# A two-layer hybrid encoder: another order of the mixer's steps, one load of x, TensorE in the order of the source

## The chip, the cores and the metric

The kernel runs on one core of a Trainium2 chip. The metric is the device time of one execution in microseconds. A core has five engines that run side by side and meet through semaphores: TensorE (PE, matrix products and transposes), VectorE (DVE), ScalarE (ACT), GpSimd (POOL) and SyncE (SP), which here only starts transfers. Products are accumulated in PSUM, in banks of 128 x 512 numbers.

## The reference

x is 256 positions of 1024 numbers. There are two layers, each of three stages, and all is float32:

```
x += 0.5 * SwiGLU(RMSNorm(x))             # FFN of width 2816
h  = RMSNorm(x); z = h @ W_in             # all projections of the mixer at once
y_att  = dilated window attention(zq, zk, zv)   # 8 heads of 64, q and k normed per head
y_pool = centred means of 2, 4, 8, 16 positions, less identity, a small map per group
y_rec  = recurrence in both directions (4 heads of 64), normed, times silu(hg)
x += concat(y_att, y_pool, y_rec) @ W_out
x += 0.5 * SwiGLU(RMSNorm(x))
```

The recurrence keeps a state S_t = diag(f_t) S_(t-1) + (1 - f_t) i_t^T with the output S_t^T q_t. Its gates f_t come from sigmoids of the projections, so the products of gates over a stretch of positions are needed.

## The kernel before

**Products.** Every product is made of three, since each number is split into a high and a low part that TensorE multiplies in full speed: high x high (L174), low x high or high x low (L175, L176). A product is 128 x 128 times 128 x 512. The weights come as halves of 512 KB in one long list, in the order of use. SP starts the transfer of a half into `stage`; ACT copies its high part `whi` (L149); DVE subtracts for the low part `wlo` (L151), or POOL does for the halves that POOL_HALVES lists. `ahead` splits a half four halves before its use, into a pool of five buffers, so that the copy of a half also waits until TensorE is done with the half five places before it.

**Stages.** An FFN goes over 11 blocks of 256 columns: `gate_up` makes gate and up for a block from four halves, `turn` transposes the product h (L352), `down` adds its part of the output. The last `down` of a stage works by quarters (dh, tt) of the residual, 128 x 512 each: six products, then DVE adds the quarter to x (`add`, L371), ACT sums its squares (L283), TensorE transposes it in four blocks (`turn`, L296, bank xps), and ACT and DVE split the transposes into `xh` (L274) and `xl` (L275) for the next stage. The turn of the last quarter is kept as `pending` and done after the first half of the next stage. The places where one stage ends and the next begins are called seams here; there are five.

**The mixer.** `mixer` runs through a string of steps, ORDER, one for each layer. c:n is chunk n of the input projection (c:2 to c:5 are q, c:6 to c:9 are k). mm:m are the products of level m of the recurrence (L541, bank lev): each level doubles the stretch over which positions meet, and up:m multiplies U and W by the gates' products in place on DVE (L520, L510), so mm of a level waits for up of the one before. put:m copies a level's result by a mask into A. ns:q scales q by its norm (DVE, L651, after the sums L644 and ACT's Ln and Exp, L645 and L646); nq:j and nk:j transpose q and k (L660, bank tp), sc and tr are the scores, pv the values' products, and o:name is a part of the output projection (L174 to L176, bank wo), the last of which goes by quarters and ends in a seam. rec and rnorm make the recurrence's output, and o:rec needs it.

**What sets the order.** SP takes its instructions in the order of the source (`manual_schedule`). For the other engines a planner orders them by its own estimate of when each will be ready, so a later-written product can stand ahead of an earlier-written transpose.

**Start.** x comes twice: as it is (for the residual) and transposed (`x_t`, four transfers of 256 KB into the space of `bias`), so that the first stage needs no transposes. In block 4 of the first FFN `setup` loads the tables of the masks and the attention bias and makes a product of them (L405, bank bps).

Of the kernel before, what the change touches and what calls it, by code (L numbers as in the profile page):

```python
# [16 lines left out]
P = 128  # L17
# [24 lines left out]
HALF = 1024  # L42
IN_NAMES = ("hq", "q", "k", "zh", "hg", "v")
OUT_NAMES = ("pool", "rec", "a0", "a1")
WIDE = ("q", "k", "zh", "v")
# [3 lines left out]
    (  # L49
# [4 lines left out]
    ),  # L54
    (
# [4 lines left out]
    ),  # L60
)
LOOK = 4
POOL_HALVES = ((3, 4, 5, 7, 8, 9, 12, 16, 20, 22, 24, 25, 27, 28, 29, 31), (2, 5, 6, 7, 8, 12, 16, 18, 19, 20, 21, 23, 24, 25, 26, 27, 28, 29, 31))
T2 = 10
FFN_HALVES = 6 * NB
# [5 lines left out]
class Trunk:  # L71
    def __init__(self, ctx, tc, x_in, xt_in, wall, prm_in, rel_in, cst_in, cst2_in, msk_in, band_in, y_out):
# [18 lines left out]
        self.pending = None  # L91
# [12 lines left out]
        self.xt0 = self.bias[:, 0]  # L104
        self.cp.tile([P, 16], F32, name="pad0")
        xr = xt_in.rearrange("p (k t) -> p k t", k=KC)
# [3 lines left out]
        for j in range(4):  # L110
            if j < 2:
                q = slice(j * HALF // 2, (j + 1) * HALF // 2)
                nc.sync.dma_start(w0[:, q], wall[0][:, q])
            nc.sync.dma_start(self.xt0[:, 2 * j:2 * j + 2, :], xr[:, 2 * j:2 * j + 2, :])
        self.feed_dma(2)
        self.prm_in, self.cst_in = prm_in, cst_in
        self.ident = self.cst[:, K_ID:K_ID + P]
        nc.scalar.dma_start(self.ident, cst_in[:, K_ID:K_ID + P])
        nc.scalar.dma_start(self.x, x_in.rearrange("p (t d) -> p t d", t=2))
# [38 lines left out]
    def ahead(self, i):  # L158

        self.feed_dma(i + LOOK + 4)  # L160
        self.feed_split(i + LOOK)

# [20 lines left out]
    def late_turn(self):  # L183

        if self.pending is not None:
            self.pending()
            self.pending = None

    def gate_up(self, i0, gu, mid=None):

        for q in range(4):
            if q == 1:
                self.late_turn()
            if q == 2 and mid is not None:
# [127 lines left out]
    def ffn(self, stage, post):  # L322
# [66 lines left out]

    def setup(self, after):  # L390
# [3 lines left out]
        mskf = self.mx.tile([P, 2 * len(LEVELS), 64], F32, tag="Kp", name="mskf", bufs=2)  # L394
        with self.tc.issue_after(after.ins):
# [53 lines left out]
    def mixer(self, l):  # L449
# [6 lines left out]
        def tl(tag, shape, dt=F32, **k):  # L456
            return mx.tile(shape, dt, tag=tag, name=tag, **k)
# [98 lines left out]
        def lev_put(m):  # L556
# [44 lines left out]
        def head_rs(sq, tag):  # L601

            ps = pg.tile([P, 512], F32, tag="g", name="hss")
            f = lambda t: t.rearrange("p a t -> p (a t)")
            hi, lo = self.split(sq)
            nc.tensor.matmul(ps, lhsT=self.bones, rhs=f(hi), start=True, stop=False)
# [5 lines left out]
            return rs  # L612

        def rec_norm():
            ops = V["ops"]
            sq = self.t2("sq")
            nc.scalar.activation(sq, ops, AF.Square)
            rs = head_rs(sq, "rrs")
            nc.vector.tensor_tensor(rs, rs, ops, op=ALU.mult)
# [162 lines left out]
        def out(nm):  # L782
# [21 lines left out]
    def body(self):  # L804
        nc = self.nc
        self.new_xt()
        for j in range(4):
            if j < 2:
                self.split_part(0, j * HALF // 2, (j + 1) * HALF // 2)
            for k in (2 * j, 2 * j + 1):  # L810
                self.parts(0, k, self.xt0[:, k, :])
# [54 lines left out]
def _pack(inp):  # L866
# [86 lines left out]
```

## Time and profile before

| | |
|---|---|
| median of three runs | 1042.7 us (1040.74 to 1046.78) |
| profiled execution | 1040.81 us, its span 1039.0 us |
| TensorE at work | 1004.4 us, 97% of the span |
| DVE, ACT, POOL | 585.0, 538.8 and 88.3 us |
| chain that ended last | TensorE 87%, DVE 6%, ACT 3%, issue 3%, DMA 1% |
| bytes moved | 182.20 MB, mean 175 GB/s |

TensorE is the engine to look at. A share of 97% includes stretches at the lower clock and a pipeline whose ends are modelled, so it is not TensorE at its peak. The waits tell where it stood, and the granted clock of a stretch tells where it was slow.

### The profile page before, as it was taken

What the parts mean: (1) busy time and instruction counts of PE and PEld (TensorE: products, weight loads), DVE (VectorE), ACT (ScalarE), POOL (GpSimd) and SP (SyncE); (2) the same over time, 40 slices, a digit from 0 to 9 for tenths busy, and PEclk for the clock granted to TensorE, in tenths of its full rate; (3) what the DMA queues carried; (4) which work ended last, traced back from release to release, by engine and by line L of the source; (5) the groups of instructions that cost most, each with busy time, mean ns of one, the idle gap of its engine ahead of it and who ended that gap; (6) DMA issues with size and microseconds to landing.
All of it is one profiled execution on the core that took longest, in us unless ns stands there. A gap on an engine that the chain in (4) does not pass through costs nothing.

```text
span 1039.0 us, 14421 instructions
## 1 busy us (share of the span) xinstructions
PE 1004.4 (97%) x5682; PEld 826.2 (80%) x5682; DVE 585.0 (56%) x776; ACT 538.8 (52%) x774; POOL 88.3 (8%) x43
## 2 busy tenths in 40 slices
PE   6999999998999999999999999999889999999998
PEld 4878888886867888888878888889768678888886
DVE  5655555669835555555565555554977155555553
ACT  7544444684865544444564444447648555444442
POOL 0000000140230000000000000004132400000000
PEclk9999999999999999999999999999989999999999
DMA  7769655553334555555555555554523346555551
GB/s 265 245 219 329 234 188 193 165 163 123 103 122 136 179 192 182 186 192 188 185 168 187 190 185 186 195 185 138 165 83 102 102 147 196 184 185 189 194 186 58
DMA packets 50420, 182.20 MB, mean 175 GB/s; under 512 B 5768, under 2 KB 6024, under 8 KB 49968
## 3 DMA queue, kind: packets, MB, share of 16 engines
q1 hardware_dynamic: 48528, 174.09, 51.6%
q0 software_dynamic: 720, 4.21, 1.1%
q10 hardware_dynamic: 1104, 2.99, 0.8%
q8 instruction: 44, 0.72, 0.3%
q14 instruction: 24, 0.20, 0.1%
HBM read 180.20 MB, written 3.16 MB: 176 GB/s over the span
## 4 chain that ended last, share of the span: by engine, by line
PE 87%; DVE 6%; ACT 3%; issue 3%; DMA 1%; POOL 0%; SPq 0%; ACTq 0%; DVEq 0%; POOLq 0%
PE gu L175 15%; PE gu L176 15%; PE gu L174 15%; PE ya L174 8%; PE ya L176 8%; PE ya L175 8%; PE hp L352 2%; PE wo L174 2%; PE wo L175 1%; PE wo L176 1%; ACT whi L149 1%; DVE wlo L151 1%; PE xps L296 1%; DMA bias<-x_t 1%; PE lev L541 1%
## 5 line engine op out<-in xcount | busy, mean ns | idle before, releaser
L149 ACT ACTIVATE whi<-stage 128x1024 fp32r<-128x1024 f32 (+1 forms) x329 | 347.1, 1056 | 395.3 <-PE gu L176 202.3
L151 DVE TENSOR_TENSOR wlo<-stage,whi 128x1024 fp32r<-128x1024 f32 (+1 forms) x294 | 360.7, 1229 | 337.5 <-ACT whi L149 337.4
L174 PE MATMUL gu<-whi,xh 128*128 128x512 f32 x704 | 275.7, 392 | 8.0 <-ACT xh L274 5.7
L175 PE MATMUL gu<-wlo,xh 128*128 128x512 f32 x704 | 274.9, 391 | 0.5 <-DVE wlo L151 0.5
L176 PE MATMUL gu<-whi,xl 128*128 128x512 f32 x704 | 274.7, 390 | 0.0
L174 PEld LDWEIGHTS gu<-whi,xh 128*128 128x128 f32 x704 | 132.5, 188 | 37.5 <-ACT xh L274 5.7
L175 PEld LDWEIGHTS gu<-wlo,xh 128*128 128x128 f32 x704 | 132.7, 189 | 28.7 <-DVE wlo L151 1.4
L176 PEld LDWEIGHTS gu<-whi,xl 128*128 128x128 f32 x704 | 132.6, 188 | 27.7
L174 PE MATMUL ya<-whi,hi 128*128 128x512 f32 x352 | 141.2, 401 | 0.0
L151 POOL TENSOR_TENSOR wlo<-stage,whi 128x1024 fp32r<-128x1024 f32 x35 | 85.0, 2437 | 654.5 <-ACT whi L149 639.2
L176 PE MATMUL ya<-whi,lo 128*128 128x512 f32 x352 | 137.8, 391 | 0.0
L175 PE MATMUL ya<-wlo,hi 128*128 128x512 f32 x352 | 137.4, 390 | 0.0
L176 PEld LDWEIGHTS ya<-whi,lo 128*128 128x128 f32 x352 | 66.1, 188 | 14.3
L175 PEld LDWEIGHTS ya<-wlo,hi 128*128 128x128 f32 x352 | 66.3, 188 | 12.4
L174 PEld LDWEIGHTS ya<-whi,hi 128*128 128x128 f32 x352 | 66.2, 188 | 12.3
L345 ACT ACTIVATE g<-gu,rc 128x256 f32<-128x256 f32 x88 | 41.5, 475 | 47.4 <-PE gu L176 47.4
L346 DVE SCALAR_TENSOR_TENSOR h<-gu,rc,g 128x256 f32<-128x256 f32 x88 | 42.0, 481 | 23.7 <-ACT g L345 23.7
L260 DVE TENSOR_TENSOR lo<-hp,hi 128x512 fp32r<-128x512 f32 x44 | 30.1, 684 | 2.8 <-ACT hi L259 2.8
L259 ACT ACTIVATE hi<-hp 128x512 fp32r<-128x512 f32 x44 | 25.6, 581 | 2.7 <-PE hp L352 2.7
L541 PE MATMUL lev<-U,W 64*64 64x64 f32 x384 | 15.6, 237 | 11.4 <-DVE W L520 11.4
L352 PEld LDWEIGHTS hp<-cst,h 128*128 128x128 f32 x176 | 21.8, 139 | 5.7
L352 PE MATMUL hp<-cst,h 128*128 128x128 f32 x176 | 26.3, 272 | 0.0
(224 smaller groups left out, 1035.8 us busy)
## 6 DMA issues: line engine op xcount, KB each, us to landing
stage<-w_all SPq DMA_DIRECT2D x327, 512.0 KB, 3.5
skew<-drow POOLq DMA_DIRECT2D x1, 2048.0 KB, 12.1
bias<-skew POOLq DMA_DIRECT2D x2, 1024.0 KB, 10.3
bias<-x_t SPq DMA_DIRECT2D x4, 256.0 KB, 7.9
x<-x ACTq DMA_DIRECT2D x1, 1024.0 KB, 8.4
band<-band ACTq DMA_DIRECT2D x1, 1024.0 KB, 8.0
y_t<-x SPq DMA_DIRECT2D x4, 256.0 KB, 2.2
stage<-w_all SPq DMA_DIRECT2D x2, 256.0 KB, 4.7
```

The source lines that it names most:

```text
L149: nc.scalar.activation(hi[:, s], st[:, s], AF.Copy)
L151: eng.tensor_tensor(lo[:, s], st[:, s], hi[:, s].bitcast(F32), op=ALU.subtract)
L174: nc.tensor.matmul(out, lhsT=ah, rhs=wh, start=start, stop=False, skip_group_check=True)
L175: nc.tensor.matmul(out, lhsT=ah, rhs=wl, start=False, stop=False, skip_group_check=True)
L176: nc.tensor.matmul(out, lhsT=al, rhs=wh, start=False, stop=stop, skip_group_check=True)
L259: self.nc.scalar.activation(hi, src, AF.Copy)
L260: self.nc.vector.tensor_tensor(lo, src, hi.bitcast(F32), op=ALU.subtract)
L296: nc.tensor.transpose(self.xps[k // 2][:, j % 2, tt * P:tt * P + P], self.x[:, tt, k * P:k * P + P], self.ident)
L345: silu = nc.scalar.activation(g2[:, tt, :], gu[tt][:, 0:256], AF.Silu, scale=r)
L346: nc.vector.scalar_tensor_tensor(h[:, tt, :], gu[tt][:, 256:512], r, g2[:, tt, :], op0=ALU.mult, op1=ALU.mult)
L352: nc.tensor.transpose(hp[:, f, tt * P:tt * P + P], h[:, tt, f * P:f * P + P], self.ident)
L541: nc.tensor.matmul(ps[d][e * 64:e * 64 + 64, hb * 64:hb * 64 + 64], lhsT=a, rhs=c, start=(hb == 0), stop=(hb == 7), skip_group_check=True)
```

## The change

1. In ORDER the steps of the mixer are placed anew: the levels are spread over more chunks, nq and nk come at other places, v's chunks come before hg's, o:rec comes last in place of o:a1, and rnorm is cut in two (rn1: squares and their split; rn2: the rest). T2, the number of buffers for small tiles, is 16.
2. x is loaded once, in quarters on SP's queue between the parts of the first half of the weights. The first stage is fed by transposes on TensorE. Twelve products of ones by ones (`idle`) stand ahead of them, the turn of the second part of x is `pending`, the squares are made later (`then`), and the halves are split no further ahead than `look`, which starts at 0.
3. TensorE is added to `manual_schedule`: its instructions keep the order of the source.
4. `setup` is cut into its loads (block 3) and its use (block 6); the tile Kp has one buffer.

```diff
-IN_NAMES = ("hq", "q", "k", "zh", "hg", "v")
-OUT_NAMES = ("pool", "rec", "a0", "a1")
+IN_NAMES = ("hq", "q", "k", "zh", "v", "hg")
+OUT_NAMES = ("pool", "a0", "a1", "rec")
...
-        "c:0 ga c:1 gb c:2 uv c:3 c:4 c:5 mm:0 ns:q put:0 mm:1 up:2 c:6 put:1 mm:2 up:4 c:7 put:2 nq:0 c:8 mm:4 up:8 nq:1 put:4 "
...
+        "c:0 ga c:1 gb c:2 uv c:3 c:4 c:5 mm:0 ns:q put:0 c:6 mm:1 up:2 put:1 nq:0 c:7 c:8 mm:2 up:4 nq:1 c:9 put:2 mm:4 up:8 ns:k "
...
-T2 = 10
+T2 = 16
...
+        for dh in range(2):
+            s = slice(dh * 512, dh * 512 + 512)
+            for tt in range(2):
+                nc.sync.dma_start(self.x[:, tt, s], xr[:, tt, s])
...
-        self.feed_split(i + LOOK)
+        self.feed_split(i + self.look)
...
+            if q == 3 and self.then is not None:
+                self.then()
+                self.then, self.look = None, LOOK
...
-            if b == min(4, NB - 1) and stage == 0:
-                self.setup(silu)
+            if b == 3 and stage == 0:
+                self.setup_loads(silu)
+            if b == 6 and stage == 0:
+                self.setup()
...
+        def rec_squares():
+            sq = self.t2("sq")
+            nc.scalar.activation(sq, V["ops"], AF.Square)
+            V["osq"] = self.split(sq)
...
+        idle = self.pg.tile([P, 512], F32, tag="g", name="idle")
+        for _ in range(12):
+            self.nc.tensor.matmul(idle[:, 0:P], lhsT=self.ones, rhs=self.ones, start=True, stop=True)
...
+        for tt in range(2):
+            self.turn(0, 0, tt)
+        self.feed_dma(5)
+
+        def second():
             for tt in range(2):
+                self.turn(0, 1, tt)
...
+        self.pending, self.then, self.look = second, sums, 0
...
-        ctx.enter_context(tc.manual_schedule(engines={mybir.EngineType.SP}))
+        ctx.enter_context(tc.manual_schedule(engines={mybir.EngineType.SP, mybir.EngineType.PE}))
```

TensorE at the seam behind layer 0's mixer, before (wo are the output projection's quarters, numbered in order; xps the banks of the transposes):

```order
L176 MATMUL wo_2839<-whi_2898,lo_2937 128x512
L174 MATMUL wo_2840<-whi_2916,hi_2936 128x512
L175 MATMUL wo_2840<-wlo_2917,hi_2936 128x512
L296 MATMUL xps_2994<-cst_85,x_83 128x128 x2
L296 MATMUL xps_2997<-cst_85,x_83 128x128 x2
L176 MATMUL wo_2840<-whi_2916,lo_2937 128x512
L296 MATMUL xps_2994<-cst_85,x_83 128x128 x2
L296 MATMUL xps_2997<-cst_85,x_83 128x128 x2
L174 MATMUL wo_2840<-whi_2916,hi_2936 128x512
L175 MATMUL wo_2840<-wlo_2917,hi_2936 128x512
L176 MATMUL wo_2840<-whi_2916,lo_2937 128x512
L174 MATMUL wo_2841<-whi_2916,hi_2936 128x512
```

and after:

```order
L175 MATMUL wo_2882<-wlo_2938,hi_2863 128x512
L176 MATMUL wo_2882<-whi_2937,lo_2864 128x512
L300 MATMUL xps_3025<-cst_85,x_83 128x128 x2
L300 MATMUL xps_3028<-cst_85,x_83 128x128 x2
L174 MATMUL wo_2883<-whi_2937,hi_2863 128x512
L175 MATMUL wo_2883<-wlo_2938,hi_2863 128x512
L176 MATMUL wo_2883<-whi_2937,lo_2864 128x512
L174 MATMUL wo_2883<-whi_2937,hi_2863 128x512
L175 MATMUL wo_2883<-wlo_2938,hi_2863 128x512
L176 MATMUL wo_2883<-whi_2937,lo_2864 128x512
L300 MATMUL xps_3025<-cst_85,x_83 128x128 x2
L300 MATMUL xps_3028<-cst_85,x_83 128x128 x2
```

Before, the transposes of the first two quarters came two products into the third quarter and one after the other; after, those of the first quarter stand behind its own sixth product (the first rows are its last), and six products later come those of the second.

TensorE in layer 1's mixer at the turn of q (tp from zq; k_ are chunks of k), before:

```order
L174 MATMUL k_6307<-whi_6183,xh_5845 128x512
L175 MATMUL k_6307<-wlo_6184,xh_5845 128x512
L176 MATMUL k_6307<-whi_6183,xl_5846 128x512
L660 MATMUL tp_6387<-cst_85,zq_6236 128x128
L660 MATMUL tp_6387<-cst_85,zq_6241 128x128
L660 MATMUL tp_6387<-cst_85,zq_6236 128x128
L660 MATMUL tp_6387<-cst_85,zq_6241 128x128
L174 MATMUL k_6306<-whi_6201,xh_5845 128x512
L175 MATMUL k_6306<-wlo_6202,xh_5845 128x512
```

and after (lev are the products of level 1):

```order
L552 MATMUL lev_6320<-U_6205,W_6206 64x64 x2
L552 MATMUL lev_6321<-W_6206,U_6205 64x64 x2
L674 MATMUL tp_6361<-cst_85,zq_6267 128x128
L674 MATMUL tp_6361<-cst_85,zq_6272 128x128
L674 MATMUL tp_6361<-cst_85,zq_6267 128x128
L674 MATMUL tp_6361<-cst_85,zq_6272 128x128
L174 MATMUL k_6300<-whi_6214,xh_5876 128x512
L175 MATMUL k_6300<-wlo_6215,xh_5876 128x512
L176 MATMUL k_6300<-whi_6214,xl_5877 128x512
```

Before, the turn followed chunk 7; now it comes between the products of level 1 and chunk 7.

ACT at that place (hs are the sums of the squares of q; L659 is Ln and L660 is Exp, L645 and L646 before), before:

```order
L149 ACTIVATE whi_6310<-stage_6156 128x1024
L643 ACTIVATE sq_6243<-zq_6241 128x512
L562 ACTIVATE A_6267<-lev_6248 128x512
L645 ACTIVATE hs_6235<-hs_6235,cols_108 128x16
L646 ACTIVATE hs_6235<-hs_6235 128x16
L149 ACTIVATE whi_6367<-stage_6181 128x1024
```

and after:

```order
L149 ACTIVATE whi_6304<-stage_6187 128x1024
L657 ACTIVATE sq_6274<-zq_6272 128x512
L573 ACTIVATE A_6298<-lev_6279 128x512
L659 ACTIVATE hs_6266<-hs_6266,cols_106 128x16
L149 ACTIVATE whi_6372<-stage_6212 128x1024
L660 ACTIVATE hs_6266<-hs_6266 128x16
```

A copy of a half, whi_6372, has come between Ln and Exp.

DVE there, before:

```order
L151 TENSOR_TENSOR wlo_6311<-stage_6156,whi_6310 128x1024
L644 TENSOR_REDUCE hs_6235<-sq_6243 128x8
L520 TENSOR_TENSOR U_6174<-U_6174,dw_6144 128x512
L520 TENSOR_TENSOR W_6175<-W_6175,dw_6144 128x512
L651 TENSOR_TENSOR zq_6236<-zq_6236,hs_6235 128x512
L651 TENSOR_TENSOR zq_6241<-zq_6241,hs_6235 128x512
```

and after:

```order
L151 TENSOR_TENSOR wlo_6305<-stage_6187,whi_6304 128x1024
L658 TENSOR_REDUCE hs_6266<-sq_6274 128x8
L151 TENSOR_TENSOR wlo_6373<-stage_6212,whi_6372 128x1024
L665 TENSOR_TENSOR zq_6267<-zq_6267,hs_6266 128x512
L665 TENSOR_TENSOR zq_6272<-zq_6272,hs_6266 128x512
L531 TENSOR_TENSOR U_6205<-U_6205,dw_6175 128x512
L531 TENSOR_TENSOR W_6206<-W_6206,dw_6175 128x512
```

The scaling of zq was behind U and W; it is now ahead of them, but behind the low part of that same half, wlo_6373.

## Rows read from the trace of the kernel before

**Rows 1.** The page: busy time, and the lines by slices.
```profile
PE 1004.4 (97%) x5682; PEld 826.2 (80%) x5682; DVE 585.0 (56%) x776; ACT 538.8 (52%) x774; POOL 88.3 (8%) x43
...
GB/s 265 245 219 329 234 188 193 165 163 123 103 122 136 179 192 182 186 192 188 185 168 187 190 185 186 195 185 138 165 83 102 102 147 196 184 185 189 194 186 58
```

**Rows 2.** TensorE's waits, whole span: microseconds in total, times, longest.
```profile
PE lev L541 <- DVE W L520: 11.4, 5, 4.5
PE gu L174 <- ACT xh L274: 5.7, 1, 5.7
PE wo L174 <- ACT hi L259: 4.5, 2, 2.2
PE xps L296 <- DVE x L371: 3.7, 5, 0.8
...
PE bps L405 <- DMA rel<-rel: 0.7, 1, 0.7
```

**Rows 3.** Timeline of a seam: start, duration, instruction, idle before it and its releaser.
```profile
325.32 0.39 PE L174 MATMUL wo<-whi,hi 128*128 128x512 f32 x1
...
326.66 1.22 DVE L151 TENSOR_TENSOR wlo<-stage,whi 128x1024 fp32r<-128x1024 f32 x1 [1.49 <-ACT whi L149]
326.68 0.39 PE L174 MATMUL wo<-whi,hi 128*128 128x512 f32 x1
...
327.80 1.28 DVE L371 SCALAR_TENSOR_TENSOR x<-wo,x 128x512 f32<-128x512 f32 x2
...
328.54 0.66 PE L296 MATMUL xps<-cst,x 128*128 128x128 f32 x4
...
331.21 0.87 DVE L275 SCALAR_TENSOR_TENSOR xl<-xps,prm,xh 128x256 fp32r<-128x256 f32 x2
...
332.08 0.40 PE L176 MATMUL wo<-whi,lo 128*128 128x512 f32 x1
...
333.26 0.66 PE L296 MATMUL xps<-cst,x 128*128 128x128 f32 x4 [0.78 <-DVE x L371]
```

**Rows 4.** TensorE's waits in the mixer of layer 0 (201.7 to 333.7).
```profile
PE lev L541 <- DVE W L520: 4.4, 3, 2.3
```

**Rows 5.** TensorE's waits in the mixer of layer 1 (708.6 to 849.8).
```profile
PE lev L541 <- DVE W L520: 7.0, 2, 4.5
...
PE lev L541 <- DVE W L510: 0.9, 1, 0.9
```

**Rows 6.** Busy time by stretches (PE, PEld, DVE, ACT, POOL); clock, DMA share, GB/s.
```profile
746.40:749.80 3.40, 3.10 (x67) 2.79 (x68) 3.33 (x6) 0.59 (x1) 0.00 (x0) 0.50 0.39 146
...
766.90:773.70 6.80, 5.21 (x72) 4.45 (x73) 5.83 (x8) 0.00 (x0) 0.89 (x1) 0.50 0.43 148
...
824.90:828.30 3.40, 3.40 (x9) 2.63 (x10) 1.22 (x2) 1.26 (x3) 0.00 (x0) 0.50 0.20 83
```

**Rows 7.** Timeline of layer 1's mixer, TensorE, DVE, ACT and POOL in order of time.
```profile
743.87 0.39 PE L176 MATMUL k<-whi,xl 128*128 128x512 f32 x1
...
744.77 0.68 DVE L644 TENSOR_REDUCE hs<-sq 128x8 f32<-128x512 f32 x1
...
745.95 1.04 ACT L149 ACTIVATE whi<-stage 128x1024 fp32r<-128x1024 f32 x1
...
746.56 1.29 DVE L651 TENSOR_TENSOR zq<-zq,hs 128x512 f32<-128x512 f32 x2
...
765.44 2.35 POOL L151 TENSOR_TENSOR wlo<-stage,whi 128x1024 fp32r<-128x1024 f32 x1 [0.40 <-ACT whi L149]
...
765.52 2.82 DVE L520 TENSOR_TENSOR W<-W,dw 128x512 f32<-128x512 f32 x1
```

**Rows 8.** Timeline of the start, TensorE.
```profile
5.75 0.80 PE L174 MATMUL gu<-whi,xh 128*128 128x512 f32 x1 [5.75 <-ACT xh L274]
...
12.52 0.42 PE L175 MATMUL gu<-wlo,xh 128*128 128x512 f32 x1
...
28.56 0.60 PE L352 MATMUL hp<-cst,h 128*128 128x128 f32 x4
```

More of the change, by code (lines that the diff above doesn't have):

```diff
@@ L71, with __init__ @@
 class Trunk:
-    def __init__(self, ctx, tc, x_in, xt_in, wall, prm_in, rel_in, cst_in, cst2_in, msk_in, band_in, y_out):
+    def __init__(self, ctx, tc, x_in, wall, prm_in, rel_in, cst_in, cst2_in, msk_in, band_in, y_out):
         self.tc, self.nc = tc, tc.nc
@@ L90, in __init__ @@
         self.cur = 0
-        self.pending = None
+        self.pending = self.then = None
+        self.look = LOOK
         self.x = self.cp.tile([P, 2, D], F32, name="x")
@@ L101, in __init__ @@
         self.qgs = self.cp.tile([P, 8], F32, name="qgs")
-        self.xt0 = self.bias[:, 0]
-        self.cp.tile([P, 16], F32, name="pad0")
-        xr = xt_in.rearrange("p (k t) -> p k t", k=KC)
+        xr = x_in.rearrange("p (t d) -> p t d", t=2)
+        self.ident = self.cst[:, K_ID:K_ID + P]
+        nc.scalar.dma_start(self.ident, cst_in[:, K_ID:K_ID + P])
         nc.scalar.dma_start(self.prm[:, 0:C_PW], prm_in[:, 0:C_PW])
@@ L109, in __init__ @@
         self.n_dma = 1
[L110 to L114, printed above, removed]
+        for dh in range(2):
+            s = slice(dh * 512, dh * 512 + 512)
+            for tt in range(2):
+                nc.sync.dma_start(self.x[:, tt, s], xr[:, tt, s])
+            if dh == 0:
+                for j in range(2):
+                    q = slice(j * HALF // 2, (j + 1) * HALF // 2)
+                    nc.sync.dma_start(w0[:, q], wall[0][:, q])
         self.feed_dma(2)
         self.prm_in, self.cst_in = prm_in, cst_in
-        self.ident = self.cst[:, K_ID:K_ID + P]
-        nc.scalar.dma_start(self.ident, cst_in[:, K_ID:K_ID + P])
-        nc.scalar.dma_start(self.x, x_in.rearrange("p (t d) -> p t d", t=2))
         self.bones = self.cp.tile([P, P], F32R, name="bones")
@@ L187, in late_turn @@
             self.pending = None
+            self.look = min(self.look + 1, LOOK)
     def gate_up(self, i0, gu, mid=None):
@@ L387, in out_part, with setup_loads @@
         self.nc.sync.dma_start(yr[:, tt, s], self.x[:, tt, s])
-    def setup(self, after):
+    def setup_loads(self, after):
         nc = self.nc
@@ L393, in setup @@
         rel = self.mx.tile([32, 8], F32, tag="rel", name="rel")
-        mskf = self.mx.tile([P, 2 * len(LEVELS), 64], F32, tag="Kp", name="mskf", bufs=2)
+        mskf = self.mx.tile([P, 2 * len(LEVELS), 64], F32, tag="Kp", name="mskf")
         with self.tc.issue_after(after.ins):
@@ L401, in setup @@
             nc.scalar.dma_start(self.band, self.band_in.rearrange("p (g s t) -> p g s t", g=4, s=2))
+        self.later = cst2, rel, mskf
+    def setup(self):
+        nc = self.nc
+        cst2, rel, mskf = self.later
         nc.vector.tensor_copy(self.msk, mskf)
@@ L577, in lev_put @@
             else:
-                V["Ao"] = tl("Kp", [P, 8, P], bufs=2)
+                V["Ao"] = tl("Kp", [P, 8, P])
                 for d in range(2):
@@ L604, in head_rs @@
             f = lambda t: t.rearrange("p a t -> p (a t)")
-            hi, lo = self.split(sq)
+            hi, lo = sq
             nc.tensor.matmul(ps, lhsT=self.bones, rhs=f(hi), start=True, stop=False)
@@ L612, in head_rs @@
             return rs
+        def rec_squares():
+            sq = self.t2("sq")
+            nc.scalar.activation(sq, V["ops"], AF.Square)
+            V["osq"] = self.split(sq)
         def rec_norm():
             ops = V["ops"]
[L616 to L618 removed]
+            rs = head_rs(V["osq"], "rrs")
             nc.vector.tensor_tensor(rs, rs, ops, op=ALU.mult)
@@ L796, in mixer @@
             "nk": lambda j: qk_turn("k", j), "sc": att_scores, "tr": att_tr, "pv": att_pv, "rec": rec_mm,
-            "rnorm": rec_norm, "o": out,
+            "rn1": rec_squares, "rn2": rec_norm, "o": out,
         }
@@ L806, in body, with sums @@
         self.new_xt()
[L807 to L811, printed above, removed]
+        idle = self.pg.tile([P, 512], F32, tag="g", name="idle")
+        for _ in range(12):
+            self.nc.tensor.matmul(idle[:, 0:P], lhsT=self.ones, rhs=self.ones, start=True, stop=True)
+        for j in range(2):
+            self.split_part(0, j * HALF // 2, (j + 1) * HALF // 2)
         self.n_split = 1
-        self.feed_split(2)
-        for dh in range(2):
+        for tt in range(2):
+            self.turn(0, 0, tt)
+        self.feed_dma(5)
+        def second():
             for tt in range(2):
-                self.squares(0, dh, tt)
+                self.turn(0, 1, tt)
+        def sums():
+            for dh in range(2):
+                for tt in range(2):
+                    self.squares(0, dh, tt)
+        self.pending, self.then, self.look = second, sums, 0
         for l in range(DEPTH):
@@ L906, in _pack @@
     x = np.ascontiguousarray(inp["x"][0].reshape(2, P, D).transpose(1, 0, 2).reshape(P, 2 * D))
-    xt = np.ascontiguousarray(inp["x"][0].T.reshape(KC, P, T).transpose(1, 0, 2).reshape(P, KC * T))
-    return x, xt, wall, prm
+    return x, wall, prm
 def _constants():
@@ L941 @@
     inp = {k: np.asarray(v) for k, v in inputs.items()}
-    x, xt, wall, prm = _pack(inp)
+    x, wall, prm = _pack(inp)
     cst, cst2, msk, band = _constants()
-    arrays = dict(x=x, x_t=xt, w_all=wall, params=prm, rel=np.ascontiguousarray(inp["rel_bias"]), cst=cst, cst2=cst2, msk=msk, band=band)
+    arrays = dict(x=x, w_all=wall, params=prm, rel=np.ascontiguousarray(inp["rel_bias"]), cst=cst, cst2=cst2, msk=msk, band=band)
     nc = bacc.Bacc("TRN2", target_bir_lowering=False, num_devices=1)
```

14 rows, old and new, of the table ORDER are left out of this document.

## The prediction

> **What bounds the kernel now.** I read the busy shares first: TensorE is at work for 97% of the 1039.0 us span [rows 1], so a change can win only in the 3% where TensorE stands or is slow, and every new wait of TensorE is paid in full. Next the waits of TensorE: they fall into few groups [rows 2]. The levels of the recurrence wait for DVE's U and W (11.4), the first product for x (5.7), the output projection for its split input (4.5 in two, one in each mixer), the transposes at the five seams between stages for the residual add (3.7), the bias product for its table (0.7). Last, for each place, the timeline or a table by stretches. The time of one product comes from the seam: starts at 325.32 and 326.68 stand six products apart [rows 3], 0.227 us each; four transposes that run as one group take about 0.41. The profiled execution took 1040.8, 1.8 more than its span; the median of the three runs is 1042.7. The sum is made against 1040.8.
>
> **The seams (dearer).** At the end of a stage each 128x512 quarter of the residual is added by DVE (L371), transposed by TensorE (L296), and split for the next stage. Before, the transposes stand some products later than the quarter that they read. From 325.32 to the last group of transposes at 333.26 there are 24 products and three groups: 24 x 0.227 + 3 x 0.41 = 6.68 of 7.94, so the seam loses 1.26 [rows 3]. After, TensorE keeps the order of the source: three of the four groups stand right behind the sixth product of their own quarter, and only the last is deferred. The waits, with before's durations: first quarter, the products end their pitch at 325.32 + 1.36 = 326.68; the add cannot start then, since a lo half (1.22) holds DVE until 327.80, and the transposes came at 328.54: 1.86. Second quarter: DVE is free, and the wait is that of the last quarter now, whose final product starts at 332.08 and whose transposes start at 333.26: 1.18 less the pitch, 0.95. Third quarter: its add stands on DVE behind another lo half and two xl (0.87 for two), which themselves wait for ACT's copies; between 0.95 and 1.86 I take 1.4. Together 4.2, against 1.26: +2.95. It happens at five seams; at the entry of layer 1's mixer the half in front of the first add belongs to POOL (half 2 is in that layer's list), so the first wait there is 0.95 and the seam +2.05. Sum 4 x 2.95 + 2.05 = **+13.9**. Bounds: all waits 0.95 gives 5 x (2.85 - 1.26) = +8; all 1.86 gives 5 x (5.58 - 1.26) = +21.6. The cover that hid the add was the next quarter's products; nothing stands in its place.
>
> **Mixer of layer 0 (cheaper).** Now the levels wait 4.4 in three waits, longest 2.3 [rows 4], and the output projection 2.2 [rows 2]: 6.6. The levels now have more chunks of products (0.227 x 12 = 2.7 each) between them, and the recurrence's output is last in the projection with its squares and split a chunk earlier, so the 2.2 goes: o:a0 and o:a1 cover it. What stays: one level wait of about 2.0 (the chain through k's evacuation still stands ahead of U and W on DVE), 0.9 at mm:128, as layer 1 shows for the same instruction [rows 5]. 6.6 - 2.9 = **-3.7**, bounds -2.5 (a second wait of 1.2 stays) and -6.
>
> **Mixer of layer 1 (no gain).** [...] The new order puts nq:0, the turn of q, directly behind mm:1; chunk 7 and mm:2, which stood ahead of it before, now follow it. TensorE must now stand at tp until zq is scaled. Before, the last product ahead of the stop starts at 743.87; the new tp stands about there less what is taken out, near 742.9. zq needs hs, which DVE ends at 744.77 + 0.68 = 745.4; then ACT takes Ln, a copy of a weight half (1.05) that now stands between Ln and Exp, and Exp; DVE takes that half's lo (1.22 [rows 3]) and only then zq [rows 7]: 745.4 + 0.3 + 1.05 + 0.2 = 747.0, the lo to 748.0 alongside, zq's two 1.29 to 749.3. The wait is 6.3. At tp for k the same chain (estimated from these rows) gives 3.1, and 5.8 if POOL's lo halves fall on U and W as they do now: W takes 2.82 there, beside 0.65 for one zq of as many numbers, while POOL's lo half runs from 765.44 [rows 7]; I take 4.3. The clock falls behind each; at the dearer price shown, 5.21/2 = 2.6 each [rows 6]. 6.3 + 4.3 + 5.2 = 15.8 stays of 16.0 (the wo wait, and the third fall behind it, go; the level waits shift to tp): about **-0.3**. Bounds: -4.5 (short second wait, falls of 1.55) and +4.1 (the second wait at 5.8, one more fall of 2.6).
> [...]
>
> **Start (about even).** Before: TensorE's first product at 5.75; the first transpose of h, with 72 products ahead of it (16.3), at 28.56: 6.5 lost besides. A product lasts 0.80 at 5.75 and 0.42 at 12.52 [rows 8], so the clock is at its lower level up to there. After: x itself is loaded in quarters and turned on TensorE; two quarters must land for the first turn, so the first product comes 1.0 later (256 KB at the first slice's 265 GB/s [rows 1]), plus 8 transposes (0.8) and the copy of the second xh (0.4): F = 8.0, bounds 7.4 and 8.6. From F the first quarter of the pass takes 3.8 (12 products of 2.7, and ACT has a square of x between its copies of xh); then 8 transposes 0.9, and the xh of the other columns at 9.5; the second and third quarter end at 11.6 and 14.3, and 24 more products put hp at F + 19.75 = 27.8: **-0.8**. The twelve filler products on the ones tile, 128 columns each, run while TensorE would stand, so they cost nothing; I assume that they raise the clock. If not, 12 products cost 0.2 more each, +2.4; at best the first quarter runs without its waits, -3.
> The rows show the clock low for the first 6.8 us of work and high after [rows 8]. [...]
>
> **Bias product.** Its tables are now loaded three blocks before they are used; the wait of 0.7 [rows 2] goes: **-0.7**. Loading x once takes 1 MB off the queues at a time when TensorE waits for the first of them only, and Kp's second buffer was not waited for: 0, at most +0.3 for a wait on the single buffer. T2 of 16 lets rnorm be split; 0.
>
> Sum: +13.9 - 3.7 - 0.3 - 0.8 - 0.7 = +8.4: 1040.8 + 8.4 = **1049.2**, 0.8% slower.
>
> **Rivals.** A, the forecast: seams pay, mixers gain little, 1049; its own range 1044 to 1056 (seams +8 and +21.6 partly cancel the other bounds). Chance 0.50; a tenth of it lies within 0.5%.
> B, the gains balance the seams: all seam waits at 0.95 (+8), layer 0 -5, layer 1 -3, start -1.5, bias -0.7: -2.2, 1038.6; with seams a little dearer, 1041. For it: the second-quarter wait shows what a free DVE does. Against: the lo half at 326.66 is in the way at four seams. Chance 0.28.
> C, on the other side, faster: the mechanism is layer 1's tp. If ACT and DVE reach zq by the time TensorE arrives (about 742.9) instead of 749.3, no wait and no fall of the clock is left in both mixers: -16.0 - 6.6 - 1.5 at start and bias, +13.9 at the seams: -10.2, 1030.6. It decides at 742.9 for zq, and likewise for zk. For it: the new order pulls the q chunks' scaling ahead of mm:2. Against: the reduce ends at 745.4 with nothing on DVE that could be dropped. Chance 0.19.
> D, the change does not do what it says at the start: the filler raises nothing, +2.4, and the clock falls once more at the seams: 1052 to 1058. Chance 0.03.
>
> The likeliest is 1049. About 0.5% (5.2 us) can be told from no change here, that is 1035.6 to 1046.0. Faster: C, 0.19. Within: B and a tenth of A, 0.33. Slower: the rest of A and D, 0.48. The range for 8 in 10 reaches up to A's end at 1056 and down to 1034, past B; it leaves out most of C and the tail of A and D.
>
> **What would show it.** Right: the waits of xps rise from 3.7 to between 14 and 28 over the span, in three waits a seam; wo's 4.5 is gone; in layer 1 tp waits 4 to 6.5 for zq twice, each followed by a stretch at clock 0.50; the first product near 8, hp near 27.8. Wrong: xps waits stay near 4 (DVE adds first, the seams are free), which makes it B or C; or tp in layer 1 finds zq ready and the clock stays at 1.00, which makes it C; or hp comes after 29, which is D.

## The result and the profile after

The changed kernel takes 1058.8 us (median, 1057.7 to 1059.2) where the kernel before takes 1041.9 (now the median of four runs): a ratio of 1.0152 with a 95% interval of 1.0118 to 1.0185. It is slower, as forecast, but by 1.5% and not 0.8%, and above the range of 1034 to 1056. The profiled execution took 1059.2 with a span of 1057.4, 18.4 over before's.

Where the 18.4 lie is read from stretches that end at the same work in both kernels, the transposes of h in the first and the last block of each FFN. A stretch between two of them that holds a mixer holds its two seams as well. The three stretches left out differ by 0.3 together.

| stretch | before | after | difference | forecast |
|---|---|---|---|---|
| start to the first hp | 28.56 | 26.86 | -1.7 | -0.8 |
| rest of the first FFN (bias product) | 161.71 | 161.05 | -0.7 | -0.7 |
| seam, mixer of layer 0, seam | 159.85 | 167.59 | +7.7 | +2.2 |
| seam between the layers | 27.97 | 31.09 | +3.1 | +2.95 |
| seam, mixer of layer 1, seam | 168.49 | 178.11 | +9.6 | +4.7 |

The two stretches with a mixer before (busy time of PE, PEld, DVE, ACT, POOL; then clock, DMA share, GB/s):

```profile
190.27:350.12 159.85, 151.23 (x1273) 124.32 (x1272) 104.98 (x190) 101.74 (x180) 38.72 (x16) 1.00 0.42 134
...
697.70:866.19 168.49, 156.71 (x1274) 128.92 (x1272) 102.79 (x179) 102.34 (x180) 46.31 (x19) 0.96 0.40 127
```

The same two after (the granted clock of the seam between the layers is 1.00 before and after):

```profile
187.91:355.50 167.59, 153.87 (x1273) 126.19 (x1272) 108.98 (x190) 101.81 (x180) 39.72 (x16) 0.98 0.40 128
...
706.33:884.44 178.11, 156.55 (x1274) 127.00 (x1272) 105.86 (x179) 102.77 (x180) 46.83 (x19) 0.96 0.38 121
```

TensorE's waits over the whole span of after, which answer to [rows 2]: in total, times, longest.

```profile
PE xps L300 <- DVE x L377: 16.4, 15, 1.7
PE tp L674 <- DVE zq L665: 5.9, 2, 5.7
PE tp L674 <- DVE zk L665: 5.3, 2, 5.2
PE lev L552 <- DVE W L531: 4.1, 1, 4.1
PE wo L174 <- ACT PT L725: 3.4, 2, 1.7
```

The transposes wait 16.4 in 15 waits, three a seam, where they waited 3.7. The two long waits at tp in layer 1 and one at level 8 in layer 0 (L552) are there as well. What the prediction did not have is the wo row: the old wait for `hi` is gone, and one of 1.7 for PT stands in each mixer instead.

The seam behind layer 0's mixer after, which answers to [rows 3] (start, duration, instruction, idle before):

```profile
328.80 0.39 PE L176 MATMUL wo<-whi,lo 128*128 128x512 f32 x1
329.01 1.22 DVE L151 TENSOR_TENSOR wlo<-stage,whi 128x1024 fp32r<-128x1024 f32 x1 [1.50 <-ACT whi L149]
330.15 0.68 DVE L377 SCALAR_TENSOR_TENSOR x<-wo,x 128x512 f32<-128x512 f32 x1
...
330.89 0.66 PE L300 MATMUL xps<-cst,x 128*128 128x128 f32 x4 [1.70 <-DVE x L377]
...
332.54 0.40 PE L176 MATMUL wo<-whi,lo 128*128 128x512 f32 x1
...
333.72 0.66 PE L300 MATMUL xps<-cst,x 128*128 128x128 f32 x4 [0.78 <-DVE x L377]
...
335.36 0.39 PE L176 MATMUL wo<-whi,lo 128*128 128x512 f32 x1
...
336.77 0.66 PE L300 MATMUL xps<-cst,x 128*128 128x128 f32 x4 [1.02 <-DVE x L377]
```

Each xps stands behind the last product of its own quarter. Less the 0.227 from one product's start to the next, the three waits are 1.86, 0.95 and 1.18; the forecast was 1.86, 0.95 and 1.4.

### The profile page after: what moved, and what is told of

It reads as the page before. It is cut to its first block, busy times and chain, and to the rows that moved or that the text cites. A ratio compares the mean times of both kernels' runs of the same rounds, so it can differ in the third digit from the quotient of the medians.

```text
span 1057.4 us, 14481 instructions
## 1 busy us (share of the span) xinstructions
PE 1011.8 (96%) x5722; PEld 831.5 (79%) x5722; DVE 592.0 (56%) x776; ACT 539.2 (51%) x774; POOL 89.8 (8%) x43
## 5 line engine op out<-in xcount | busy, mean ns | idle before, releaser
L175 PEld LDWEIGHTS ya<-wlo,hi 128*128 128x128 f32 x352 | 66.4, 189 | 12.4
L300 PE MATMUL xps<-cst,x 128*128 128x128 f32 x96 | 14.9, 281 | 16.4 <-DVE x L377 16.4
L300 PEld LDWEIGHTS xps<-cst,x 128*128 128x128 f32 x96 | 10.6, 141 | 23.2 <-DVE x L377 22.7
```

Of the source, the lines that this page charges most:

```text
L175: nc.tensor.matmul(out, lhsT=ah, rhs=wl, start=False, stop=False, skip_group_check=True)
L300: nc.tensor.transpose(self.xps[k // 2][:, j % 2, tt * P:tt * P + P], self.x[:, tt, k * P:k * P + P], self.ident)
```

## The experiments

Ratios are to the kernel before, run beside each of them, with the 95% interval. "The base" is e4_start.

**TensorE ordered by the planner again (e1_planner).**

```diff
-        ctx.enter_context(tc.manual_schedule(engines={mybir.EngineType.SP, mybir.EngineType.PE}))
+        ctx.enter_context(tc.manual_schedule(engines={mybir.EngineType.SP}))
```

> The changed kernel with one thing undone: TensorE is taken out of manual_schedule again, so the planner orders it; the new ORDER, start and setup stay. Theory 1 (the fixed order of TensorE costs the time, at the seams and by holding it at tp for zq and zk): the xps waits fall from 16.4 to 3 to 5 us, the tp waits of 11.2 fall under 3 with one fall of the clock less, and the time comes to 1036 to 1043. Rival (the new ORDER costs the mixers their time whoever orders TensorE): only the seams come back, -12 to -13, 1045 to 1047, and the sum of TensorE's waits in the two mixers without xps stays near 20.

1037.8 us, 0.9957 (0.9940 to 0.9975). TensorE's waits:

```profile
PE tp L674 <- DVE zk L665: 4.7, 1, 4.7
PE tp L674 <- DVE zq L665: 4.3, 1, 4.3
...
PE xps L300 <- DVE x L377: 3.7, 5, 0.8
```

The time is theory 1's, but of the waits only a part: xps is back at 3.7, while tp still waits 9.0 in layer 1 and the mixers' waits without xps come to 16.8, nearer the rival's 20. So the fixed order of TensorE costs 20 to 21 us, and the turns' places in ORDER cost their waits under either rule.

**The old ORDER, TensorE still fixed (e2_oldorder).** ORDER, IN_NAMES and OUT_NAMES of before in the changed kernel:

```diff
-IN_NAMES = ("hq", "q", "k", "zh", "v", "hg")
-OUT_NAMES = ("pool", "a0", "a1", "rec")
+IN_NAMES = ("hq", "q", "k", "zh", "hg", "v")
+OUT_NAMES = ("pool", "rec", "a0", "a1")
...
+        "c:0 ga c:1 gb c:2 uv c:3 c:4 c:5 mm:0 ns:q put:0 mm:1 up:2 c:6 put:1 mm:2 up:4 c:7 put:2 nq:0 c:8 mm:4 up:8 nq:1 put:4 "
...
+        "rn1 rn2 c:17 tr:6 tr:7 c:18 c:19 o:pool pv:0 pv:1 pv:2 o:rec pv:3 o:a0 o:a1 "
```

> The changed kernel with ORDER, IN_NAMES and OUT_NAMES of before (rn1 and rn2 where rnorm stood, one behind the other); TensorE still in the order of the source, new start and setup. Theory 1 (TensorE's fixed order makes the seams dear, the new ORDER is roughly neutral): xps waits stay at 15 to 17, the mixers' own waits are 15 to 20 us as in the kernel before or a little more, time 1052 to 1057. Rival (the new ORDER is what costs the mixers): the mixers come back to before's waits or better, time 1050 or less. A third possibility: old ORDER was written for a planner, and in source order its steps wait more (tr, rec and hss stand directly behind what they need): over 1062.

1058.7 us, 1.0153 (1.0122 to 1.0184), from 1055.5 to 1060.4: as slow as the change. xps waits 16.3, as expected; hss now waits 4.9 for the split that is written just ahead of it, and tp 3.2. The time lies between theory 1's and the third possibility's. With TensorE fixed neither ORDER is the better.

**The turns one quarter later (e3_late).**

```diff
+            if (dh, tt) != (0, 0):
+                self.turn(stage, *divmod(2 * dh + tt - 1, 2))
             if (dh, tt) == (1, 1):
                 self.pending = lambda: self.turn(stage, dh, tt)
-            else:
-                self.turn(stage, dh, tt)
```

> The changed kernel, where each quarter's turn at a seam is written behind the six products of the next quarter instead of its own (the last stays pending). Theory 1 (the wait is the add's latency of 0.95 to 1.9 with nothing of TensorE behind it): six products are 1.36 of cover, so the first wait falls to 0.3 to 0.5, the others to 0 to 0.3; xps waits fall from 16.4 to 2 to 4, time 1045 to 1048. Rival (the later turn only moves the wait to the next stage's first products, which need xh and xl): gu and ga wait for xh or xl 1.5 to 3 a seam, time 1055 or more.

1045.6 us, 1.0033 (1.0017 to 1.0050).

```profile
PE gu L174 <- DVE xl L279: 2.2, 3, 0.7
PE gu L174 <- ACT xh L278: 1.7, 2, 1.5
PE ga L167 <- DVE xl L279: 1.5, 2, 0.7
PE xps L300 <- DVE x L377: 1.3, 4, 0.3
```

xps fell to 1.3, and about 4 of new waits for xl and xh came at the next stage's first products (the row for xh holds 1.3 of the start). Theory 1 holds with a small part of the rival: by the medians 13.2 us of the change's loss (12.4 by the ratios) was the transposes' place at the seams.

**The start and the setup alone (e4_start, run again as e9_start_again).** e2_oldorder with the planner for TensorE: before, with the new start, the cut setup and T2 of 16.

> The kernel before with the new start (x loaded once, filler, turns on TensorE) and the cut setup alone: ORDER and names of before, the planner orders TensorE. Theory 1 (start -1.7 and bias -0.7 are real and independent of the rest): first transpose of h at 26.5 to 27.5, time 1038 to 1040.5. Rival (the start's gain needs TensorE in source order, since the planner moves transposes or filler): first transpose of h at 28 or later, time 1041 to 1044.

1031.0 us, 0.9890 (0.9866 to 0.9916), far below the forecast of both. The first hp came at 26.58, as expected; but the mixer stretches fell too, to 158.4 and 162.6, and the wait of wo was gone. That pointed to something in the change, other than the start, that helps the mixers under the old order.

> The kernel of e4_start once more, as the base of the three beside it. Both theories: 1029 to 1033.

1030.5 us, 0.9878 (0.9857 to 0.9899).

**More small buffers (e5_t2).** The kernel before with T2 at 16 and, as in the change, one buffer for Kp:

```diff
-T2 = 10
+T2 = 16
...
-                V["Ao"] = tl("Kp", [P, 8, P], bufs=2)
+                V["Ao"] = tl("Kp", [P, 8, P])
```

> The kernel before with the small-tile pool T2 at 16 instead of 10 (Kp with one buffer, as in the change), nothing else. Theory 1 (the output projection's wait for rnorm's split, 2.2 in each mixer, comes from the tenth buffer: the low part of rnorm's squares cannot be written until pv has read an older tile of the pool): the wo waits of 4.5 vanish, in layer 1 the fall of the clock behind it (1.7 lost) too, time 1034 to 1037. Rival (the wait is the length of rnorm's chain, and it was the split of rnorm or the old product order that moved it): the wo waits stay at 3 to 4.5, time 1040 to 1043.

1034.7 us, 0.9929 (0.9907 to 0.9951): theory 1. Before, ACT had written the high part of rnorm's squares, the input of the low part, by 296.73, but DVE stood idle ahead of the low part until pv was done:

```profile
305.17 0.91 DVE L260 TENSOR_TENSOR lo<-sq,hi 128x512 fp32r<-128x512 f32 x1 [8.34 <-PE pv L721]
```

With 16 buffers the same instruction runs 11 us earlier:

```profile
293.78 0.86 DVE L260 TENSOR_TENSOR lo<-sq,hi 128x512 fp32r<-128x512 f32 x1 [3.43 <-ACT hi L259]
```

The wo wait vanished from the waits, and the stretch of layer 1 fell from 168.5 to 162.8, that of layer 0 from 159.9 to 156.7. The idle time of an engine that is not the bottleneck (8.34 behind "PE pv", with the input long ready) was the sign of a missing buffer.

**tr:7 earlier (e6_tr7).** On e3_late, in both layers:

```diff
-c:18 pv:0 tr:5 tr:6 "
-        "c:19 rn2 tr:7 pv:1 o:pool
+c:18 pv:0 tr:5 tr:6 tr:7 "
+        "c:19 rn2 pv:1 o:pool
```

> The changed kernel with the turns at the seams one quarter later (e3_late) and, in both layers, tr:7 moved from behind rn2 to in front of c:19. Theory 1 (o:pool's fourth bank waits for ACT's copy PT of the turn tr:7, which stands on ACT behind the chain of hg's gate): the two waits of wo for PT (3.4) go, time 1041 to 1043, 3 to 4 under e3_late. Rival (ACT is late there anyhow, and the wait moves to pv or to o:a0's inputs): 1045 to 1046, with pv or wo waiting 1.5 or more in each mixer.

1046.4 us, 1.0045 (1.0028 to 1.0061), no gain on e3_late: the rival.

```profile
PE wo L174 <- ACT hi L263: 3.2, 2, 1.6
```

The wait for PT went, and one of the same size came at o:a0, for the high part (`hi`) of pv. On ACT that copy stands right behind rnorm's, which itself waits for DVE:

```profile
311.11 0.63 ACT L263 ACTIVATE hi<-rrs 128x512 fp32r<-128x512 f32 x1 [1.18 <-DVE rrs L634]
311.64 1.06 ACT L263 ACTIVATE hi<-pv 128x512 fp32r<-128x512 f32 x2
```

The theory fell in the sum: tr:7's PT is only the first thing that is late on ACT there.

**The turns of q and k later in layer 1 (e7_l1).** On e3_late:

```diff
-c:6 mm:1 up:2 put:1 nq:0 c:7 c:8 mm:2 up:4 nq:1
+c:6 mm:1 up:2 put:1 c:7 c:8 nq:0 mm:2 up:4 nq:1
...
-c:10 put:4 nk:0 c:11 mm:8 up:16 put:8 nk:1 c:12
+c:10 put:4 c:11 mm:8 up:16 put:8 nk:0 c:12 nk:1
```

> The changed kernel with the late turns of e3_late and, in layer 1 alone, nq:0 written behind c:8 instead of ahead of c:7, nk:0 behind mm:8, nk:1 behind c:12. Theory 1 (TensorE stands at tp for zq and zk because the turns come before DVE has scaled them; with two chunks more they are ready, and a level wait of 1 to 3 takes part of it back): tp waits fall from 11.2 to under 2, the clock falls at most once, time 1036 to 1040. Rival (U and W come behind zq and zk on DVE, so the levels wait as long as the turns did, as in the kernel before): lev waits of 7 to 10 in layer 1, time 1043 to 1046.

1039.4 us, 0.9978 (0.9967 to 0.9988), 6.2 under e3_late. Waits of layer 1's mixer:

```profile
PE tp L674 <- DVE zk L665: 3.0, 2, 2.4
PE tp L674 <- DVE zq L665: 2.5, 2, 2.2
```

The tp waits fell from 11.2 to 5.5, not under 2, and the stretches at half clock from 6.8 each to 3.4. The levels did not take the wait back: they wait 1.6 there. The turns' place was the cause of the half that went. In what stays, POOL has a part: DVE's two steps for zq take 3.47 beside a low half of POOL from 748.42 to 750.78, where they took 1.29 in the changed kernel.

**A chunk more before level 8 in layer 0 (e8_l0).** On e3_late:

```diff
-c:10 mm:8 up:16 put:8 nk:0 c:11 nk:1 c:12 mm:16
+c:10 c:11 mm:8 up:16 put:8 nk:0 c:12 nk:1 mm:16
```

> The changed kernel with the late turns of e3_late and, in layer 0 alone, c:11 ahead of mm:8 (nk:0 and nk:1 a chunk later). Theory 1 (level 8 waits 4.1 for U and W because the two sums for zk and two low halves stand ahead of them on DVE; a chunk of 2.9 covers most of it and the clock does not fall): the wait falls to about 1.2, time 1040.5 to 1043. Rival (the copies of the halves are themselves released by the products of the chunk that TensorE is held from, so U and W become later by the same chunk): the wait stays at 3 to 4, time 1045 to 1047.

1047.1 us, 1.0055 (1.0036 to 1.0074), 1.5 over e3_late: the rival's time, but not its mechanism. The wait at level 8 fell from 4.1 to 1.4, as theory 1 had it, and one of 2.6 came at level 16. There a low half of DVE had fallen beside one of POOL and took 3.09 in place of 1.22, with the next U and W behind it:

```profile
252.50 0.27 PE L552 MATMUL lev<-U,W 64*64 64x64 f32 x2 [1.35 <-DVE W L531]
...
253.80 2.40 POOL L151 TENSOR_TENSOR wlo<-stage,whi 128x1024 fp32r<-128x1024 f32 x1 [13.69 <-ACT whi L149]
...
254.19 3.09 DVE L151 TENSOR_TENSOR wlo<-stage,whi 128x1024 fp32r<-128x1024 f32 x1
...
260.07 0.27 PE L552 MATMUL lev<-U,W 64*64 64x64 f32 x2 [2.63 <-DVE W L531]
```

So the waits are 4.0 together where they were 4.1, and the half clock behind the second is 6.8, where e3_late has 3.4. That the chunk would pay without POOL's half there is not shown.

**No filler (e10_nofill).** The base without the twelve `idle` products.

> The kernel of e4_start without the twelve filler products. Theory 1 (the filler raises the clock before the first product): the first products run at half the clock, first transpose of h 1.5 to 3 later, time 1.5 to 3 above the base. Rival (the filler changes nothing, since the start is bound by x's arrival and ACT's copies): within 0.7 of the base.

1033.7 us, 0.9906 (0.9887 to 0.9925), 3.2 over the base, with intervals that overlap (the base again: 0.9857 to 0.9899). The first products without the filler:

```profile
7.98 0.79 PE L174 MATMUL gu<-whi,xh 128*128 128x512 f32 x1 [1.33 <-ACT xh L278]
8.57 0.63 PE L175 MATMUL gu<-wlo,xh 128*128 128x512 f32 x1
```

and in the base with it (e9_start_again):

```profile
8.29 0.50 PE L174 MATMUL gu<-whi,xh 128*128 128x512 f32 x1 [0.44 <-ACT xh L278]
8.63 0.40 PE L175 MATMUL gu<-wlo,xh 128*128 128x512 f32 x1
```

Without the filler the products start 0.59 and then 0.43 apart, as in the kernel before; with it, 0.34 and then 0.23. hp came at 27.95 instead of 26.10: 1.9 of the 3.2, within the 1.5 to 3 of theory 1. Another 1.0 lies in layer 1's mixer, where a stretch of 3.4 at half clock came that the base does not have (743.6 to 746.9); that the filler has to do with it is not shown.

**Values before the gate, recurrence last, on the base (e11_names).**

```diff
-        "rn1 rn2 c:17 tr:6 tr:7 c:18 c:19 o:pool pv:0 pv:1 pv:2 o:rec pv:3 o:a0 o:a1 "
+        "rn1 c:17 tr:6 tr:7 c:18 c:19 rn2 o:pool pv:0 pv:1 pv:2 pv:3 o:a0 o:a1 o:rec "
```

> The kernel of e4_start with v's chunks in front of hg's, o:rec last in the output projection and rn2 behind c:19; the other steps stay as in ORDER of before, the planner orders TensorE. Theory 1 (hg's chunks last put the gate's chain and rnorm on ACT and DVE at the head of the output projection, where PT and the splits of pv queue behind them): wo or pv waits of 1 to 2.5 appear in each mixer, time 2 to 5 above the base. Rival (this part is neutral or a gain, and the new places of the levels and turns alone cost the mixers): within 1 of the base or below it.

1032.0 us, 0.9891 (0.9869 to 0.9914), 1.5 over the base, with ranges that overlap. wo waits 1.3 over both mixers, less than theory 1 said. Whether this part costs 1 or 2 us or nothing stays open.

**Two halves off POOL, on the base (e12_pool).** In layer 1:

```diff
-(2, 5, 6, 7, 8, 12, 16, 18, 19, 20, 21,
+(2, 5, 6, 7, 8, 12, 16, 20, 21,
```

> The kernel of e4_start with halves 18 and 19 of layer 1's mixer taken from POOL and given to DVE. Theory 1 (U and W for level 8 take 1.85 and 2.82 because POOL's low half shuts DVE out): U and W take 0.7 each, the level's wait of 4.1 to 4.5 falls by 1.5 to 3 although DVE has two low halves more, one stretch of half clock (3.4) goes, time 2 to 5 below the base. Rival (DVE's added low halves of 1.22 stand ahead of U and W and take the gain): within 1.5 of the base.

1025.5 us, 0.9839 (0.9815 to 0.9863): theory 1, and the fastest kernel of this study. DVE at level 8:

```profile
757.62 1.23 DVE L151 TENSOR_TENSOR wlo<-stage,whi 128x1024 fp32r<-128x1024 f32 x1 [0.84 <-ACT whi L149]
...
759.96 0.68 DVE L531 TENSOR_TENSOR W<-W,dw 128x512 f32<-128x512 f32 x1
```

and in the base (e9_start_again), beside POOL's halves:

```profile
759.56 2.82 DVE L531 TENSOR_TENSOR W<-W,dw 128x512 f32<-128x512 f32 x1
```

W takes 0.68, and so does U, where they took 2.82 and 1.85, and W ends 1.7 earlier although a low half of 1.23 stands ahead. The wait at level 8 fell from 4.5 to 1.9 and the half clock behind it from 6.8 to 3.4. But a stop of 2.5 at level 2, which the base has too (2.4), now met 3.4 at half clock where the base has none, so layer 1's half clock is 6.8 in both. The stretch of layer 1 fell from 162.6 to 160.3. The profiled spans differ by 2.8 (1028.7 and 1025.9), 2.4 of it in that stretch. The rest of the 5 us between the medians goes with the clock: the runs of e12_pool go from 1029.8 at a mean granted clock of 0.993 to 1023.8 at 1.000, those of the base from 1031.2 at 0.993 to 1029.1 at 0.997. Whether the edit makes such falls rarer is not shown.

Put in a row, by the ratios: 16 buffers -7.4 us; new start and setup -4 to -5 more (2.3 to 2.8 by the stretches); the new ORDER +7 to +8; TensorE in the order of the source +20.

## Why the prediction was wrong

**Right: the seams.** Forecast +13.9. The transposes wait 12.7 more, and the one seam that stands alone lost 3.1 for a forecast 2.95. At the entry of layer 1's mixer, where the first add was to find DVE free, they wait 2.6 and not 3.4. e3_late returns 12 to 13.

**Right: start, filler and bias.** The first product came at 8.18 for a forecast 8.0, hp at 26.86 for 27.8, so the gain is 1.7 and not 0.8; the bias wait is gone. e10_nofill bears out that the filler helps: without it hp comes 1.9 later. That TensorE's clock is low at first was my inference from how long a product takes. What the trace of before shows is the spacing: products start 0.43 apart from 10.38 to 12.52, as they do at a granted clock of 0.50 (826.07 to 827.35), and 0.23 apart later (15.60 to 15.83). The granted clock of those first stretches is given as 1.00, before (5.5 to 12.6) and after (8.0 to 14.9).

**Right: the waits at tp.** Forecast 6.3 and 4.3, measured 5.7 and 5.2. For zq, ACT takes the copy of a half between Ln and Exp, and DVE a low half ahead of zq, as the order had it:

```profile
756.62 1.04 ACT L149 ACTIVATE whi<-stage 128x1024 fp32r<-128x1024 f32 x1
...
757.69 1.23 DVE L151 TENSOR_TENSOR wlo<-stage,whi 128x1024 fp32r<-128x1024 f32 x1 [1.32 <-ACT whi L149]
758.83 1.29 DVE L665 TENSOR_TENSOR zq<-zq,hs 128x512 f32<-128x512 f32 x2
```

For zk the prediction stood between 3.1 and 5.8 and took 4.3. The dearer case came: POOL's halves fell on U and W, as before the change, and zk stood behind them, from 780.52:

```profile
774.93 2.38 POOL L151 TENSOR_TENSOR wlo<-stage,whi 128x1024 fp32r<-128x1024 f32 x1 [6.41 <-ACT whi L149]
...
776.00 1.85 DVE L531 TENSOR_TENSOR U<-U,dw 128x512 f32<-128x512 f32 x1
...
777.70 2.35 POOL L151 TENSOR_TENSOR wlo<-stage,whi 128x1024 fp32r<-128x1024 f32 x1 [0.39 <-ACT whi L149]
777.78 2.82 DVE L531 TENSOR_TENSOR W<-W,dw 128x512 f32<-128x512 f32 x1
```

**Wrong: "so the 2.2 goes: o:a0 and o:a1 cover it".** The old wait went, and a new one came in its place. For the old one T2 is enough, which the prediction costed at 0 ("T2 of 16 lets rnorm be split; 0"): e5_t2 has the old order, loses both waits and is 7.5 faster, the largest gain in the change. So the prediction had counted this gain, but under the new order and not under T2; whether the new order with ten buffers would have removed the waits too, no run shows. What came is o:pool's, 1.7 in each mixer. With TensorE in source order, tr:7 stands ahead of o:pool with only pv:1 between, and holds the bank that o:pool's last quarter needs until ACT has copied PT:

```profile
309.75 0.63 ACT L646 ACTIVATE hgt<-hgt 128x512 f32<-128x512 f32 x1 [0.76 <-DVE hgt L645]
...
311.99 0.63 ACT L263 ACTIVATE hi<-rrs 128x512 fp32r<-128x512 f32 x1 [0.66 <-DVE rrs L634]
312.52 0.58 ACT L725 ACTIVATE PT<-tp 128x512 f32<-128x512 f32 x1
...
313.15 0.51 PE L174 MATMUL wo<-whi,yh 128*128 128x512 f32 x1 [1.67 <-ACT PT L725]
```

ACT takes PT behind the gate's chain (hgt, L646) and the split of rnorm, which the new order puts there. e6_tr7 showed that PT's place alone is not the cause: what is late behind rnorm's split changes, and the wait stays. That hg's chunks in the last place are the cause was not shown (e11_names). With the planner the two waits together are 0.5 (e1_planner), so they come with TensorE's fixed order.

**Wrong: the size of layer 0's level wait.** Forecast 2.0 and no fall of the clock; it was 4.1, with a fall. DVE had two low halves and, in lines left out, two sums for zk (L658) and two steps for the turn of q (L684) ahead of U and W:

```profile
248.83 1.23 DVE L151 TENSOR_TENSOR wlo<-stage,whi 128x1024 fp32r<-128x1024 f32 x1 [0.46 <-ACT whi L149]
...
252.52 1.23 DVE L151 TENSOR_TENSOR wlo<-stage,whi 128x1024 fp32r<-128x1024 f32 x1 [1.00 <-ACT whi L149]
...
254.85 0.68 DVE L531 TENSOR_TENSOR W<-W,dw 128x512 f32<-128x512 f32 x1
```

Six instructions of others, and idle time between for ACT's copies, then U and W. With the planner this wait is 3.9, so the new order makes it and not TensorE's. I took 2.0 from a wait of before [rows 4]; I should have added up DVE's queue in the new order, as I did for zq. The other term that was to stay in layer 0, 0.9 at mm:128, came out by luck: the 0.9 of [rows 5] is no wait of mm:128 but one of level 1's products for the first W (L510 is in the step uv, not in up). Behind the stop of 4.1 the clock fell, and in layer 1 it fell twice (busy time of the engines by stretch; clock, DMA share, GB/s):

```profile
254.80:261.60 6.80, 6.01 (x76) 5.21 (x77) 6.80 (x12) 1.67 (x3) 0.00 (x0) 0.50 0.46 151
...
756.50:763.30 6.80, 3.51 (x10) 2.77 (x11) 5.58 (x9) 2.21 (x5) 0.00 (x0) 0.50 0.49 158
...
780.40:787.20 6.80, 5.70 (x15) 4.49 (x16) 2.74 (x5) 0.60 (x1) 0.00 (x0) 0.50 0.21 78
```

In layer 0 that is 6.01 of TensorE at a clock of 0.50, where products start 0.43 apart (259.27 to 260.98) and not 0.23: about half of it, 3.0, is lost, which the prediction did not have. How much of it a run pays varies: the same stop of 4.1 met 3.4 at half clock in e3_late and not 6.8. In layer 1 it is 3.51/2 + 5.70/2 = 4.6, for a forecast 5.2.

**The sum.** The 16.0 from which the forecast for layer 1 counts are 7.0 and 0.9 at the levels [rows 5], 2.2 at wo [rows 2] and half of the 3.10, 5.21 and 3.40 of TensorE's time at a granted clock of 0.50 [rows 6]. Layer 0: waits without xps of 6.9 where 2.9 were forecast (wo 1.7 and level 2.1 more, 0.2 small), and 3.0 of clock: 7.0 more, of which 5.5 show in the stretch. Layer 1: 15.4 of waits where 10.6 were forecast (wo 1.7, sc 1.5 and level 1.0 are new, the turns 0.6 over), 0.6 less of clock: 4.2 more, 4.9 in the stretch. The two stretches are 10.4 over; the start's gain of 0.9 and some tenths elsewhere make that the 10 us between 8.4 and 18.4.

e1_planner parts this in two. With the planner the new order leaves layer 0's stretch at 159.9, as before, so the forecast gain of 3.7 is not there even without the fixed order. TensorE's fixed order then adds 7.7 in layer 0 and 10.0 in layer 1, where the seams were to cost 5.9 and 5.0. The level and sc waits are there in e1_planner too, so they come with the new order; the wo waits, 0.5 there, come with TensorE's.

So two steps failed: in each mixer the gain of 2.2 at wo was booked whole, without the wait that came next at the same bank; and layer 0's level wait was put at 2.0 and its fall of the clock at nothing. One slip besides: the lower bound for layer 1, worked out from its own terms (6.3 + 3.1 + 2 x 1.55 against 16.0), is -3.5 and not -4.5.

## What to carry to other kernels

Before TensorE is fixed to the order of the source, the source must already hold the slack that a planner would add: a transpose written right behind the products that it reads pays the latency of the engines between at every repetition: here 16.4 in 15 waits, where it had been 3.7 in five. When a wait is to be removed, add up the queue of the engine that releases it in the new order, and look at which buffer or bank is next: here six more small buffers gave 7.5 us, as much as the new order of the steps lost. Look also at what a second engine does at the very place where the chain is waiting: U and W on DVE took 4.7 beside POOL's low halves and 1.4 without them.

## What the runs showed of the hardware

How long the clock stays down could not be told from the length of the stop. The stop of 4.1 at level 8 of layer 0 met 6.8 us at half clock in the changed kernel and in e7_l1, and 3.4 in e3_late and e6_tr7; one of 2.6 at level 16 met 6.8 in e8_l0. A stop of 2.5 us at level 2 of layer 1 met 3.4 us in e12_pool and none in the base (2.4). So a difference of a few us between two medians can be the clock's, and is better read from the stretches.

Twelve products of 128 columns whose result nobody reads were worth about 2 us: with them TensorE's real products start 0.23 apart from the second on, at 8.63 in the base; without them they start 0.43 apart up to 12.84 (e10_nofill). In the changed kernel, behind a stop of 1.13 between the transposes and the first product at 8.18, the products still take 0.39 to 0.50, and not the 0.53 to 0.79 of e10_nofill. The spacing is shown; that the clock makes it is my inference.

U and W (L531 on DVE, layer 1) took 4.7 beside POOL's low halves and 1.4 without them. In the changed kernel POOL's halves end at 777.31 and 780.05, U at 777.85 and W at 780.60: each of the two steps ends 0.54 or 0.55 behind POOL's, about as long as one takes alone (0.68). The trace shows the durations and the ends, and not what holds the steps up. In e12_pool it was worth more to let DVE do two halves of 1.23 itself than to wait for POOL's: 2.3 us in the stretch of layer 1.
